# Gated linear attention: the state's products with the queries on four quarters of the array, a gate exponential put behind the next tile's decay logarithm, and the last output scaling on VectorE alone

## The chip, the cores and the metric

The kernel runs on one core of a Trainium2 chip. Its engines are TensorE (PE; PEld is its load of weights), VectorE (DVE), ScalarE (ACT), GpSimd (POOL) and SyncE (SP, which only issues DMAs here). The metric is the device time of one execution in microseconds: 2154.04 us before the change, the median of three runs (2153.7 to 2154.69).

## The reference

One layer of a decoder with two groups of heads side by side, for 2048 prompt tokens and 8 x 8 sample tokens: sliding-window attention (group A), gated linear attention (GLA, group B: 4 heads, key width 64, value width 128), an output projection, and a squared-ReLU MLP of width 4096, with RMSNorm before and after both halves. Cut to the part that the change touches:

```python
b = jnp.cumsum(log_a, axis=chunk)             # decays, within a chunk
k_rel = exp(where(causal, b_t - b_s, -inf)) * k_s
o_intra = einsum(einsum(q, k_rel), v)         # inside a chunk
q_dec, k_dec, a_blk = q * exp(b), k * exp(b_last - b), exp(b_last)
def step(S, xs):
    o = einsum('bthk,bhkv->bthv', q_dec, S)   # state times queries
    S = a_blk * S + einsum('bthk,bthv->bhkv', k_dec, v)
o = rms_norm(o_intra + o_inter, g_gla) * silu(gr)
...
x = x + rms_norm(f, g_ffn_post)               # the end of the layer
```

All inputs and outputs are float32.

## The kernel before

The work is cut into 16 tiles of 128 prompt tokens and one of 64 sample tokens, and goes in stages: the input projection of group A with its attention, GLA with its own input projection, the output projection, and two halves of the MLP, up and down, for 1024 tokens each. Large products are split into high and low parts that go through the array as fp32r, three products each; the small products of GLA are plain f32, and each of those leaves two matmul records in the trace.

**The GLA stage.** `gla(i, gp, og)` (from L1217) is a generator for tile i. Between its steps it yields a number of fill products; the loop at its caller then runs that many matmuls of the next tiles' projection (`gproj`), or of the output projection (`out`) at the end, from one list, so TensorE has work while the other engines prepare the tile. `G_FILL = (34, 14, 16, 8, 20)` gives these numbers. TensorE keeps the order in which the program issues its products.

For one tile, in the order of the program:

- `qk_T` (L1106) transposes queries and keys into PSUM bank "d". DVE copies the keys to `kt`; ACT copies the queries, scaled, into `qz`, which has two planes: plane r holds the queries of head r of a pair in 64 of 128 partitions, and zeros in the other 64.
- After 34 fills, seven `level_sums` (L1150) build decay sums on ACT (exponentials into `dec`) and DVE (sums in `before` and `after`), one for each of the block lengths 1 to 64; `weighted` (L1129) multiplies them into keys `XK` and queries `XQ`. The last level is issued behind the previous tile's masked copies (`put`). `dec[:, NL]` is the exponential of the whole tile's cumulated decay.
- `decayed(i + 1)` (L1210) starts the next tile: `log_decays` (L976) computes a small product z and on ACT its Abs, Exp and Ln.
- After 14 fills, `gate` (L1091) makes silu of the output gate: Abs, Exp and Ln on ACT, a DVE instruction, a last Exp on ACT (L1099), and two products on POOL.
- After 16 fills the decayed keys are transposed into bank "e" and copied by ACT to `kd`; then 8 fills.
- The scores of all levels (`gl`, `gh`), on two column halves of the array, then `ds`, the state's increment, also on two column halves, into bank "d". DVE computes `qd = qz * dec[:, NL]` (L1272), zeros included, copies the scores under masks into `AH`, and both engines copy them to `AT`. DVE updates the state S into its other buffer.
- After 20 fills, the output `o` in bank "e": for each head one product of `qd` (128 partitions, half of them zeros) and the state of its pair of heads, added to one product of `AT` and the values:

```python
o_ = bank([P, 4, P], "e", f"o_{i}")
for h in range(4):
    if i > 0:
        te.matmul(o_[:, h, :], qd[:, h % 2, h // 2], So[:, h // 2], start=True, stop=False)
    te.matmul(o_[:, h, :], AT[:, h, :], gv[:, h * P : (h + 1) * P], start=i == 0, stop=True)
```

- `finish_out` (L1178) squares, normalizes and gates `o` during the next tile, transposes it and stores it.

Most ACT and DVE instructions here are ordered by a scheduler when the program is built; `tc.issue_after(x)` puts those inside the block behind x on its engine.

**The end.** The last four token tiles leave their second halves ready (`prepare_last`). For each tile the last product is added to `f` (L2081); `square_last` (L2147) squares it on ACT and multiplies it by the gain; `finish_last` (L2155) makes the root on ACT (Ln, Exp), scales and adds the residual (L2165), and stores 512 columns at a time (L2166). The very last tile is handled in two pieces of 256 columns: the left piece is multiplied by the gain on POOL (L2151), scaled on ACT (L2162), added on POOL (L2163) and stored from ACT's queue (L2168); DVE and SP do the rest.

Of the kernel before, what the change touches and what calls it, by code (L numbers as in the profile page):

```python
# [15 lines left out]
AF = mybir.ActivationFunctionType  # L16
ALU = mybir.AluOpType
# [4 lines left out]
P = 128  # L22
# [3 lines left out]
NB = T // P  # L26
# [15 lines left out]
NL = len(LEVELS)  # L42
# [110 lines left out]
def hybrid_step_kernel(ctx: ExitStack, tc: tile.TileContext, I, O):  # L153
    nc = tc.nc
# [15 lines left out]
    def y_rows(i):  # L170
        return yp[i * P : (i + 1) * P, :] if i < NB else ys

    te, ac, dv = (InOrder(tc, engine) for engine in (nc.tensor, nc.scalar, nc.vector))
# [4 lines left out]
    def bank(shape, kind, name):  # L178

        return ps.tile(shape, F32, tag=kind, name=name, bufs=1 if kind in "de" else 2)  # L180
# [241 lines left out]
    half_of = slice(HD), slice(HD, P)  # L422
# [462 lines left out]
    for i in range(NB):  # L885
# [21 lines left out]
        if i >= NB - 2:  # L907
            t = i - NB + 2
# [60 lines left out]
    def ranks_T(pair, out):  # L969
        te.transpose(out, f32(glr[:, pair]).rearrange("p a r -> p (a r)"), ident)  # L970
        return out

    def first_ranks():
        ac.activation(glrT_first, ranks_T(0, bank([P, P], "b", "pg_0")), AF.Copy)

    def log_decays(i, z, t, gt, out):  # L976
        for g in range(2):
            te.matmul(z[:, g], wgk[:, i % 2, g * P : (g + 1) * P], gt[:, : z.shape[2]], start=True, stop=True)
        nc.scalar.activation(t, z, AF.Abs)
        nc.scalar.activation(t, t, AF.Exp, scale=-1.0)  # L980
        if out is not None:
            nc.scalar.activation(out, t, AF.Ln, bias=1.0)
        return z

    def first_decays():
# [44 lines left out]
    def places(name, shape, n=1, kind=F32):  # L1030
        return cycle([sp.tile(shape, kind, name=f"{name}{u}") for u in range(n)])
# [7 lines left out]
    XK = sp.tile([P, NL, 2, P], F32, name="XK")  # L1039
    XQ = sp.tile([P, NL, 2, 2, P // 2], F32, name="XQ")  # L1040
    sgs, prs = places("sg", [P, 512]), places("pr", [P, 256])
    qds = places("qd", [P, 2, 2, P])
    decs = places("dec", [P, NL + 1, 2, P])
    befores, afters = places("before", [P, 2, P]), places("after", [P, 2, P])
    kts = places("kt", [P, 2, P], 2)
# [45 lines left out]
    def gate(i, gp, n):  # L1091

        gr = gp[:n, 1024:1536]
        t = next(sgs) if n == P else s_sg
        nc.scalar.activation(t[:n], gr, AF.Abs)
        nc.scalar.activation(t[:n], t[:n], AF.Exp, scale=-1.0)
        nc.scalar.activation(t[:n], t[:n], AF.Ln, bias=1.0)
        nc.vector.scalar_tensor_tensor(t[:n], gr, 0.0, t[:n], op0=ALU.min, op1=ALU.subtract)
        nc.scalar.activation(t[:n], t[:n], AF.Exp)  # L1099
        engine = nc.vector if i in (0, NB) else nc.gpsimd  # L1100
        engine.tensor_tensor(t[:n], t[:n], gr, op=ALU.mult)
        t4 = t[:n].rearrange("p (h d) -> p h d", h=4)
        engine.tensor_tensor(t4, t4, ggla[:n].unsqueeze(1).to_broadcast([n, 4, P]), op=ALU.mult)
        return t
# [112 lines left out]
    def gla(i, gp, og=iter(())):  # L1217

        assert {(i, 0), (i, 1)} <= projected
        before, after = pre.pop(i)
        next(og, None)
        kt = qk_T(i, gp, P)
        dec = next(decs)
        following = decayed(i + 1) if i < NB - 1 else iter(())
        yield G_FILL[0] + 3 * (i == 1) if i else G_FIRST_FILL, True
        deque(og, 0)
        put_diagonal(i, AH, gp, P)
        for l, b in enumerate(LEVELS):  # L1230
            if l < (4 if i == 2 else NL - 1) or i == 0:
                level_sums(before, after, dec, l, b)
            else:
                with tc.issue_after(put[0].ins):
                    level_sums(before, after, dec, l, b)
            if l == NL - 1:
                kd = next(kds)
                pair = i // 2 + 1 if i % 2 == 0 and i < NB - 2 else 0
                turned = keys_decayed(after, kt, next(kdTs), P, "e", kd, pair)
                nc.scalar.activation(dec[:, NL], before, AF.Exp, scale=1.0 / 16)  # L1240
            weighted(XK, XQ, dec, kt, qz, l, b)
        next(turned)
        deque(following, 0)
        yield G_FILL[1] - 3 * (i == 1), True
        assert {(i, c) for c in range(4)} <= projected
        sg = gate(i, gp, P)
        yield G_FILL[2], True
        deque(turned, 0)
        yield G_FILL[3], True
        low = bank([P, 4, 4, P // 4], "c", f"gl_{i}")  # L1250
        high = bank([P, 512], "c", f"gh_{i}")
        mid = high[:, :256].rearrange("p (l h q) -> p l h q", l=2, h=4)
        far = high[:, 256:384].rearrange("p (r q) -> p r q", r=2)
        levels = [*(low[:, l] for l in range(4)), *(mid[:, l] for l in range(2))]
        for l, gm in enumerate(levels):
            for g in range(2):
                keys = XK[:, l, g] if l else kt[:, g]
                for u, uu in enumerate(half_of):
                    te.matmul(
                        gm[uu, 2 * g : 2 * g + 2], keys[:, uu], XQ[:, l, :, g, u * 32 : u * 32 + 32], start=True, stop=True  # L1260
                    )
        for g in range(2):
            te.matmul(far[half_of[g]], XK[:, NL - 1, g, :HD], XQ[:, NL - 1, :, g], start=True, stop=True)
        gv = gp[:, 512:1024]
        ds = bank([P, 2, P], "d", f"ds_{i}")
        for h in range(4):
            te.matmul(
                ds[half_of[h % 2], h // 2], kd[:, h * HD : (h + 1) * HD], gv[:, h * P : (h + 1) * P],
                start=True, stop=True,
            )  # L1270
        qd = next(qds)
        nc.vector.tensor_tensor(qd, qz, dec[:, NL].unsqueeze(1).to_broadcast([P, 2, 2, P]), op=ALU.mult)  # L1272
        for l, gm in enumerate(levels):
            put_level(AH, gm, msk[:, l], LEVELS[l])
        for g in range(2):
            nc.scalar.activation(AT[:HD, 2 * g : 2 * g + 2, HD:], far[half_of[g]], AF.Copy)
        put[:] = [nc.vector.tensor_copy(AT[half_of[1], :, half_of[1]], AH[half_of[1]])]
        done = nc.scalar.activation(AT[half_of[0], :, half_of[0]], AH[half_of[0]], AF.Copy)
        put.append(done)
        So, Sn = S[i % 2], S[(i + 1) % 2]  # L1280
        with tc.issue_after(put[0].ins):
            for g in range(2):
                nc.vector.scalar_tensor_tensor(
                    Sn[:, g], So[:, g], dec[:, NL, g, P - 1 : P], ds[:, g], op0=ALU.mult, op1=ALU.add
                )
        yield G_FILL[4], True
        o_ = bank([P, 4, P], "e", f"o_{i}")
        for h in range(4):
            if i > 0:
                te.matmul(o_[:, h, :], qd[:, h % 2, h // 2], So[:, h // 2], start=True, stop=False)  # L1290
            te.matmul(o_[:, h, :], AT[:, h, :], gv[:, h * P : (h + 1) * P], start=i == 0, stop=True)
        with tc.issue_after(done.ins):
            next(wo_parts, None)
        ogs_of[i] = og = finish_out(i, lambda h: o_[:, h, :], sg, P, "e")
        if i == NB - 1:
            yield from og
            for g in range(2):
                for r in range(2):
                    nc.sync.dma_start(O["gla_prompt"][0, 0, 2 * g + r], Sn[half_of[r], g])
# [847 lines left out]
    def square_last(i, fi, cc):  # L2147
        x1, fg, ssq = ending[i]
        left = cc.start == 0 and cc.stop < 512
        squares(i, fi[:, cc], cc, ssq[:, 1:2] if left else ssq[:, 0:1])  # L2150
        (nc.gpsimd if left else nc.vector).tensor_tensor(fg[:, cc], fi[:, cc], gpost[:, cc], op=ALU.mult)  # L2151
        if left:
            nc.vector.scalar_tensor_tensor(ssq[:, 2:3], ssq[:, 1:2], 1.0 / D, ssq[:, 2:3], op0=ALU.mult, op1=ALU.add)

    def finish_last(i):  # L2155
        x1, fg, ssq = ending[i]
        nc.scalar.activation(ssq[:, 3:4], ssq[:, 0:1], AF.Ln, scale=1.0 / D, bias=ssq[:, 2:3])
        nc.scalar.activation(ssq[:, 3:4], ssq[:, 3:4], AF.Exp, scale=-0.5)
        parts = [two, one]
        if i == NB - 1:  # L2160
            parts, left = [two, slice(256, 512)], slice(0, 256)
            nc.scalar.activation(fg[:, left], fg[:, left], AF.Copy, scale=ssq[:, 3:4])  # L2162
            nc.gpsimd.tensor_tensor(fg[:, left], fg[:, left], x1[:, left], op=ALU.add)  # L2163
        for dd in parts:
            nc.vector.scalar_tensor_tensor(fg[:, dd], fg[:, dd], ssq[:, 3:4], x1[:, dd], op0=ALU.mult, op1=ALU.add)  # L2165
            nc.sync.dma_start(y_rows(i)[:, dd], fg[:, dd])  # L2166
        if i == NB - 1:
            nc.scalar.dma_start(y_rows(i)[:, left], fg[:, left])  # L2168

    latest, newest = [], []  # L2170

# [277 lines left out]
```

## Time and profile before

| | |
|---|---|
| median of 3 runs | 2154.04 us |
| the profiled execution | 2154.72 us |
| its span | 2152.9 us |
| PE busy, matmul records | 2142.2 us, 11854 |
| PEld busy | 1860.6 us |
| DVE busy | 1528.0 us |
| ACT busy | 1220.5 us |
| POOL busy | 263.0 us |
| GLA stage, from the first tile's scores to the last tile's output | about 328 to 673 us |

The profile shows one execution. Busy time is the time in which an engine had at least one instruction at work; matmuls overlap, so a busy PE is not PE at its peak, and the distance from one start to the next says more than the length of one record. The chain of waits goes back from the last instruction to what released it, or to the instruction before it on its engine. In a row of a timeline stand the start, the length, the engine, the line, the operation, the tiles (out<-in), the shape and the count.

### The profile page before, as it was taken

The page shows a single profiled execution, that of the slowest core. Times are in us where ns is not written, and L with a number is a line of the kernel's source. Part 1 is how long each engine was busy: PE and PEld are TensorE (multiplying, and loading weights), DVE is VectorE, ACT ScalarE, POOL GpSimd, SP SyncE. Part 2 cuts the span into 40 slices and gives each one's busy share as a digit, 9 for nine tenths or more (in the row PEclk, how much of TensorE's full clock was granted, in tenths as well). Part 3 has the DMA queues.
Part 4 walks back from the last instruction along what each step waited for, and adds up shares of the span by engine and source line. Part 5 has one row for each costly group of instructions (what it writes and reads, how often), then busy time and mean ns, then how long its engine had stood idle before and what let it go on. Part 6 is the DMA issues. An engine that isn't in the chain of part 4 may idle for free.

```text
span 2152.9 us, 34347 instructions
## 1 busy us (share of the span) xinstructions
PE 2142.2 (100%) x11854; PEld 1860.6 (86%) x11854; DVE 1528.0 (71%) x3184; ACT 1220.5 (57%) x2628; POOL 263.0 (12%) x424
## 2 busy tenths in 40 slices
PE   9999999999999999999999999999999999999998
PEld 9999999999998888888888888888888888888887
DVE  7998878777775666988887555548766666555576
ACT  7998867566664444655555544345444445544454
POOL 4676511111111100000000000000000000000000
PEclk9999999999999999999999999999999999999999
DMA  7444341243427567777776877668544443766685
GB/s 243 157 145 145 103 118 46 86 138 114 157 100 272 189 207 240 247 258 274 260 274 218 263 246 224 209 199 275 176 170 162 152 158 125 260 204 192 193 273 177
DMA packets 241468, 411.55 MB, mean 191 GB/s; under 512 B 24893, under 2 KB 143405, under 8 KB 237181
## 3 DMA queue, kind: packets, MB, share of 16 engines
q1 hardware_dynamic: 240988, 408.95, 57.5%
q8 instruction: 94, 1.54, 0.3%
q14 instruction: 82, 0.66, 0.1%
q10 hardware_dynamic: 304, 0.40, 0.1%
HBM read 265.82 MB, written 143.99 MB: 190 GB/s over the span
## 4 chain that ended last, share of the span: by engine, by line
PE 96%; ACT 1%; DVE 1%; DMA 0%; issue 0%; POOL 0%; SPq 0%; DVEq 0%; POOLq 0%; ACTq 0%
PE dn L142 28%; PE gproj L142 13%; PE uc L142 8%; PE uX L142 8%; PE out L1423 7%; PE proj L142 6%; PE ud L142 4%; PE ue L142 4%; PE ub L142 4%; PE sam L142 2%; PE dsam L142 1%; PE o L142 1%; PE sc L142 1%; PE pT L142 1%; PE av L142 1%; PE gl L142 1%
## 5 line engine op out<-in xcount | busy, mean ns | idle before, releaser
L142 PE MATMUL dn<-o0t,o0s 128*128 128x512 f32 x888 | 345.4, 389 | 0.4 <-DVE f L2081 0.4
L142 PE MATMUL dn<-o0t,o1s 128*128 128x512 f32 x888 | 345.6, 389 | 0.0
L142 PE MATMUL dn<-o1t,o0s 128*128 128x512 f32 x888 | 345.5, 389 | 0.0
L2067 DVE TENSOR_TENSOR o1s<-rs,o0s 128x512 fp32r<-128x512 f32 x224 | 154.6, 691 | 222.4 <-ACT o0s L2066 219.4
L2066 ACT ACTIVATE o0s<-rs 128x512 fp32r<-128x512 f32 x224 | 141.2, 631 | 291.5 <-PE dn L142 255.8
L142 PE MATMUL gproj<-wg,gxh 128*128 128x384 f32 x1024 | 271.3, 341 | 0.2 <-ACT dec L1156 0.2
L142 ACT ACTIVATE st<-st 128x512 f32<-128x512 f32 x224 | 141.1, 630 | 101.7 <-DVE st L142 96.9
L142 PEld LDWEIGHTS dn<-o0t,o0s 128*128 128x128 f32 x888 | 166.8, 188 | 36.6 <-DVE f L2081 0.8
L142 PEld LDWEIGHTS dn<-o1t,o0s 128*128 128x128 f32 x888 | 166.7, 188 | 35.2
L142 PEld LDWEIGHTS dn<-o0t,o1s 128*128 128x128 f32 x888 | 166.7, 188 | 34.9
L142 PE MATMUL uc<-H,s 128*128 128x512 f32 x768 | 186.5, 391 | 0.0
L142 PEld LDWEIGHTS gproj<-wg,gxh 128*128 128x128 f32 x1024 | 183.8, 188 | 2.8 <-issue 1.9
L142 PE MATMUL gproj<-wg,gxl 128*128 128x384 f32 x576 | 185.9, 341 | 0.0
L142 PE MATMUL uX<-H,w 128*128 128x512 f32 x768 | 185.1, 390 | 0.0
L142 PEld LDWEIGHTS uX<-H,w 128*128 128x128 f32 x768 | 144.0, 188 | 30.3
L142 PEld LDWEIGHTS uc<-H,s 128*128 128x128 f32 x768 | 143.0, 188 | 30.6 <-ACT st L142 0.2
L1423 PE MATMUL out<-wo,mt 128*128 128x512 f32 x680 | 158.6, 392 | 0.0
L218 POOL TENSOR_TENSOR frs<-rs_v,half 128x1 f32<-128x1 f32 (+1 forms) x13 | 12.3, 952 | 1197.2 <-DVE rs_v L216 1197.2
L2067 DVE TENSOR_TENSOR o1t<-rt,o0t 128x512 fp32r<-128x512 f32 x222 | 152.1, 686 | 5.4 <-ACT o0t L2066 5.4
L1423 PEld LDWEIGHTS out<-wo,mt 128*128 128x128 f32 x680 | 126.5, 188 | 26.1
L2066 ACT ACTIVATE o0t<-rt 128x512 fp32r<-128x512 f32 x222 | 137.0, 619 | 10.9 <-DMA rt<-t_d 7.1
L142 DVE TENSOR_TENSOR st<-st 128x512 f32<-128x512 f32 x160 | 110.7, 692 | 30.1 <-ACT st L142 25.8
(440 smaller groups left out, 4314.3 us busy)
## 6 DMA issues: line engine op xcount, KB each, us to landing
s_d<-st SPq DMA_DIRECT2D x32, 1792.0 KB, 8.5
rs<-s_d SPq DMA_DIRECT2D x224, 256.0 KB, 3.4
raw<-in_w_up SPq DMA_DIRECT2D x64, 512.0 KB, 5.0
rt<-t_d SPq DMA_DIRECT2D x128, 256.0 KB, 3.8
rt<-in_w_down SPq DMA_DIRECT2D x96, 256.0 KB, 2.9
t<-in_w_down SPq DMA_DIRECT2D x64, 256.0 KB, 3.7
t_d<-t SPq DMA_DIRECT2D x32, 512.0 KB, 5.6
h_d<-ht SPq DMA_DIRECT2D x8, 1280.0 KB, 7.6
```

The source lines that it names most:

```text
L142: ins = call(*a, **k)
L218: return nc.gpsimd.tensor_tensor(out, v[:n], e, op=ALU.pow)
L1423: te.matmul(banks[c], x, w[:, c * 512 : (c + 1) * 512], start=k + u == 0, stop=k == KT - 1 and u == len(products) - 1,)
L2066: high = nc.scalar.activation(hi, raw, AF.Copy)
L2067: low = nc.vector.tensor_tensor(lo, raw, f32(hi), op=ALU.subtract)
```

## The change

Three things, all in the code printed above.

1. The products of state and queries. `qd` loses its zero half: DVE now makes it with two instructions, one for each 64 partitions, right behind `gate`. The products are eight of 64 x 64 (row half r is the head within a pair, column half u is half of the tokens, g the pair of heads), and stand behind `ds`, ahead of the 20 fills. Heads of row half 0 accumulate in bank "e", those of row half 1 in the second half of the bank "d" in which `ds` lies (`fourth`). The products of `AT` stay where they were and add to both. The transposes of `qk_T` move from bank "d" to "c".
2. Order on ACT and DVE. In tiles 1 to 14 the gate's last Exp is put behind the Ln of the latest `log_decays`. The last two levels, no longer only the last, are issued behind the previous tile's masked copies.
3. The end. The gain's product of the last tile is made once, 512 wide, on DVE, and the last scaling and store are as in the other tiles: two scalings and two stores of 512 columns, none on ACT or POOL.

```diff
@@ log_decays
-            nc.scalar.activation(out, t, AF.Ln, bias=1.0)
+            logged[:] = [nc.scalar.activation(out, t, AF.Ln, bias=1.0)]
@@ 
-    qds = places("qd", [P, 2, 2, P])
+    qds = places("qd", [P, 2, P])
@@ gate
-        nc.scalar.activation(t[:n], t[:n], AF.Exp)
+        with tc.issue_after(logged[0].ins) if 0 < i < NB - 1 else nullcontext():
+            nc.scalar.activation(t[:n], t[:n], AF.Exp)
@@ gla
-        kt = qk_T(i, gp, P)
+        kt = qk_T(i, gp, P, "c")
...
-            if l < (4 if i == 2 else NL - 1) or i == 0:
+            if l < (4 if i == 2 else NL - 2) or i == 0:
...
         sg = gate(i, gp, P)
+        qd = next(qds)
+        for r, rr in enumerate(half_of):
+            nc.vector.tensor_tensor(qd[rr], qz[rr, r], dec[rr, NL], op=ALU.mult)
...
-        ds = bank([P, 2, P], "d", f"ds_{i}")
+        fourth = bank([P, 4, P], "d", f"ds_{i}")
+        ds = fourth[:, :2]
...
-        qd = next(qds)
-        nc.vector.tensor_tensor(qd, qz, dec[:, NL].unsqueeze(1).to_broadcast([P, 2, 2, P]), op=ALU.mult)
+        So, Sn = S[i % 2], S[(i + 1) % 2]
+        o_ = bank([P, 2, P], "e", f"o_{i}"), fourth[:, 2:]
+        for g in range(2):
+            for u, uu in enumerate(half_of):
+                for r, rr in enumerate(half_of):
+                    if i > 0:
+                        te.matmul(
+                            o_[r][uu, g], qd[rr, g, uu], So[rr, g], start=g == 0, stop=False, skip_group_check=True
+                        )
...
         yield G_FILL[4], True
-        o_ = bank([P, 4, P], "e", f"o_{i}")
         for h in range(4):
-            if i > 0:
-                te.matmul(o_[:, h, :], qd[:, h % 2, h // 2], So[:, h // 2], start=True, stop=False)
-            te.matmul(o_[:, h, :], AT[:, h, :], gv[:, h * P : (h + 1) * P], start=i == 0, stop=True)
+            te.matmul(
+                o_[h % 2][:, h // 2], AT[:, h, :], gv[:, h * P : (h + 1) * P], start=i == 0, stop=True, skip_group_check=True
+            )
...
-        ogs_of[i] = og = finish_out(i, lambda h: o_[:, h, :], sg, P, "e")
+        ogs_of[i] = og = finish_out(i, lambda h: o_[h % 2][:, h // 2], sg, P, "e")
@@ square_last
-        (nc.gpsimd if left else nc.vector).tensor_tensor(fg[:, cc], fi[:, cc], gpost[:, cc], op=ALU.mult)
         if left:
             nc.vector.scalar_tensor_tensor(ssq[:, 2:3], ssq[:, 1:2], 1.0 / D, ssq[:, 2:3], op0=ALU.mult, op1=ALU.add)
+        else:
+            nc.vector.tensor_tensor(fg[:, one], fi[:, one], gpost[:, one], op=ALU.mult)
@@ finish_last
-        parts = [two, one]
-        if i == NB - 1:
-            parts, left = [two, slice(256, 512)], slice(0, 256)
-            nc.scalar.activation(fg[:, left], fg[:, left], AF.Copy, scale=ssq[:, 3:4])
-            nc.gpsimd.tensor_tensor(fg[:, left], fg[:, left], x1[:, left], op=ALU.add)
-        for dd in parts:
+        for dd in (two, one):
...
-        if i == NB - 1:
-            nc.scalar.dma_start(y_rows(i)[:, left], fg[:, left])
```

More of the change, by code (lines that the diff above doesn't have):

```diff
@@ L971, in ranks_T @@
         return out
+    logged = []
     def first_ranks():
@@ L1279, in gla @@
         put.append(done)
-        So, Sn = S[i % 2], S[(i + 1) % 2]
         with tc.issue_after(put[0].ins):
```

## The prediction

> **What bounds the kernel now.** I read the page first, then the busy time of the engines in the stretch that the change touches, then TensorE's own waits there, and last the chain of waits and the order of single matmuls in one tile.
>
> ```profile
> span 2152.9 us, 34347 instructions
> ...
> PE 2142.2 (100%) x11854; PEld 1860.6 (86%) x11854; DVE 1528.0 (71%) x3184; ACT 1220.5 (57%) x2628; POOL 263.0 (12%) x424
> ...
> PE 96%; ACT 1%; DVE 1%; DMA 0%; issue 0%; POOL 0%; SPq 0%; DVEq 0%; POOLq 0%; ACTq 0%
> ```
>
> TensorE (PE) is busy over the whole span and holds 96% of the chain that ended last. The profiled execution took 2154.72 us, 1.8 more than its span and 0.68 above the median of 2154.04; I make the sum as a difference and take it off the median. The stretch of gated linear attention, 328 to 673 us:
>
> ```profile
> 328.00:673.00 345.00, 344.96 (x2972) 331.50 (x2971) 264.39 (x787) 220.56 (x659) 60.58 (x60) 1.00 0.37 124
> ```
>
> ```profile
> PE gproj L142 <- ACT dec L1156: 0.2, 1, 0.2
> ```
>
> The first row gives the busy time of PE, PEld, DVE, ACT and POOL in these 345 us, then the granted clock of 1.00; the second is the only wait of PE from 320 to 680. PE is busy for 344.96 us, VectorE (DVE) for 264 and ScalarE (ACT) for 221. So an edit here is worth what it takes off PE's own stream, and edits on DVE and ACT are worth nothing unless they let PE wait.
>
> **What the state product costs now.** One tile in the chain of waits (start, length, matmul records; an f32 matmul leaves two):
>
> ```profile
> 509.89 0.70 PE gproj L142 x4
> 510.59 1.08 PE gl L142 x32
> ...
> 512.36 0.44 PE ds L142 x8
> 512.80 3.67 PE gproj L142 x20
> 516.47 1.78 PE o L142 x16
> ```
>
> A tile's o group is four products of state and queries and four of AT and values, 16 records in 1.78 us: 0.111 us a record. The eight of the state take 0.89 us. They run in 15 tiles (tile 0 has no state), which the count confirms:
>
> ```profile
> L142 PE MATMUL o<-S,qd 128*128 128x128 f32 x120 | 23.1, 274 | 0.0
> ```
>
> 120 records in 15 tiles are 15 x 0.89 = 13.4 us of PE. (The 23.1 us of this row counts overlapping records twice over with those of AT; the spacing is what counts.)
>
> **What it costs after.** Each tile gets eight products of 64 rows by 64 columns with 128 moving columns: two pair groups g, on four quarters of the array. That is 16 records, four for each quarter. What quarters do is read from neighbours that use halves:
>
> ```profile
> 510.08 0.51 PE L142 MATMUL gproj<-wg,gxh 128*128 128x384 f32 x2
> 510.52 0.45 PE L142 MATMUL gl<-XQ,kt 128*64 128x64 f32 x8
> 510.80 0.87 PE L142 MATMUL gl<-XQ,XK 128*64 128x64 f32 x24
> 511.50 0.86 PE L142 MATMUL gh<-XQ,XK 128*64 128x64 f32 x20
> 512.19 0.61 PE L142 MATMUL ds<-gp,kd 128*64 128x128 f32 x8
> 512.73 0.45 PE L142 MATMUL gproj<-wg,gxl 128*128 128x384 f32 x1
> 513.01 0.51 PE L142 MATMUL gproj<-wg,gxh 128*128 128x384 f32 x2
> ```
>
> ds is eight records of 128 columns on two column halves, and the chain above gives them 0.44 us: 0.109 us for a round of two, as long as a full-array record takes alone. So column halves run side by side. Four side by side are seen in the sample's scores, which lie on four column strips of 32:
>
> ```profile
> 283.00 0.44 PE L142 MATMUL ssc<-kc,qs 64*32 64x128 f32 x8
> 283.24 0.31 PE L142 MATMUL ssc<-kns,qs 64*32 64x64 f32 x8
> 283.48 0.45 PE L142 MATMUL gproj<-wg,gxl 128*128 128x384 f32 x1
> ```
>
> From 283.00 to 283.48 there are eight records of 128 columns and eight of 64. One after another they would need 8 x 0.109 plus 8 x 0.058 (the 24 gl records take 0.70 from 510.80 to 511.50, 0.058 a round) = 1.34 us; in rounds of four 2 x 0.109 + 2 x 0.058 = 0.33, and the 0.48 that passed hold a change of mode too. So strips work as four independent streams. If quarters do the same, the 16 records are four rounds: 4 x 0.109 = 0.44 us. What the trace doesn't show is two row halves at once; that is the main uncertainty.
>
> A change of array shape costs something as well. In the group above gproj follows gproj by 0.175 us (four in 0.70 in the chain), so after the pair that starts at 510.08 gl would follow at 510.43; it starts at 510.52, 0.09 later. Its first eight records take 0.28 us where the later ones take 0.233, another 0.05. Out of it, ds should end at 512.19 + 0.44 = 512.63; gproj starts at 512.73, and its next one 0.28 later where 0.175 is usual, 0.10 twice. Now ds (128 x 64) would be followed by quarters (64 x 64), a switch more in each tile; the way back to gproj is paid already. The same two shapes follow each other once, in the other direction:
>
> ```profile
> 372.23 0.68 PE L142 MATMUL s_oi<-s_at,gp_s 64*64 64x64 f32 x16
> 372.84 0.29 PE L142 MATMUL s_oe<-s_qz,s 128*64 128x16 f32 x4
> ```
>
> s_oi is 16 records of 64 columns, eight rounds of 0.058 and 0.05 for the first: its end is at 372.23 + 0.52 = 372.75, and s_oe starts at 372.84, 0.09 later. So I price the switch at 0.09 plus 0.05 for the first round, 0.14 us; bounds 0.09 (no slow first round) and 0.20 (as the way back to gproj).
>
> The Trainium skill, page "TensorEngine Tiling (Array Packing)", section "Tiling Modes", says that changing the tiling mode, not just the tile, drains TensorE; this speaks against the change. The trace agrees, with the 0.09 us at each of these places, and its drain is in the sum.
>
> Per tile: 0.89 off, 0.44 + 0.14 on, 0.31 us gained; over 15 tiles 4.7 us. With the bounds of the switch 3.8 to 5.4 us. Another bound: a round of gl takes 0.058 us, loads of 64 weight columns included; if the loads of the two row halves queue in one column half, a round of quarters takes 2 x 0.058 = 0.117 instead of 0.109, 0.5 us over all tiles.
>
> **Does PE wait anywhere new?** The quarters stand right behind ds, ahead of the 20 fill products (3.67 us) that stood before them. They need qd, the state, and the banks. The state was written in the tile before. qd is on DVE:
>
> ```profile
> L1272 DVE TENSOR_TENSOR qd<-qz,dec x16: 678/689/693, 326.1 to 655.1; 128x512 f32<-128x512 f32 x16
> ```
>
> ```profile
> L1135 DVE TENSOR_TENSOR XQ<-dec,qz x73: 415/422/445, 436.6 to 654.8; 128x256 f32<-128x256 f32 x73
> ```
>
> One instruction of 0.69 us becomes two of half the size, 0.69 to 0.84 together by these rows, and stands behind the gate in the tile, 24 fill products ahead of its use; DVE idles 80 us in the stretch. Cost nothing; if it came late, PE would wait for its length at most. The bank of o's first half held the transposed decayed keys, which ACT copies out to kd before ds anyway:
>
> ```profile
> 533.05 0.36 ACT L1146 ACTIVATE kd<-kdT 128x256 f32<-128x256 f32 x1
> ```
>
> ```profile
> 533.67 0.61 PE L142 MATMUL ds<-gp,kd 128*64 128x128 f32 x8
> ```
>
> In this tile the copy ends at 533.41 and ds starts at 533.67: 0.26 us of room, the tightest place that I found. The change reorders two things ahead of that copy on ACT. The gate's last exponential goes behind the next tile's decay logarithm:
>
> ```profile
> 526.22 0.63 ACT L1099 ACTIVATE sg<-sg 128x512 f32<-128x512 f32 x1 [0.28 <-DVE sg L1098]
> ```
>
> Here ACT idled 0.28 us for DVE's part of the gate while that logarithm stood behind it. After the change the logarithm runs first, so the level sums start earlier by up to the 0.63 us of that exponential, and the copy with them; queued behind the exponential on ACT are the level exponentials, and POOL waits for it with the gate's two products, which the next tile's output scaling needs. Also one level more of the sums is put behind the masked copies. Both give room, so I take nothing. AT is safe too:
>
> ```profile
> 515.57 0.40 ACT L1278 ACTIVATE AT<-AH 64x256 f32<-64x256 f32 x1
> ```
>
> ```profile
> 516.52 0.39 PE L142 MATMUL o<-gp,AT 128*128 128x128 f32 x2
> ```
>
> AT is ready at 515.97 and first used at 516.52. With the quarters ahead (0.58 us) and the first two state records gone (0.22 us), it is used 0.36 us later after ds than now. The transposes of queries and keys go from bank d to c, whose last readers are done before AT. Bank d, which now keeps o's second half, is next taken by the following decay product, and that stands on PE behind the transposes of the scaled output, so behind o's last reader. None of this adds a wait to PE.
>
> **The tail.** It is a chain without PE. For the third last tile and the last two:
>
> ```profile
> 2141.34 1.42 DVE L2165 SCALAR_TENSOR_TENSOR lfg<-lfg,lssq,lx 128x512 f32<-128x512 f32 x2 [0.63 <-ACT lssq L2158]
> ```
>
> ```profile
> 2144.83 1.89 DVE L2165 SCALAR_TENSOR_TENSOR lfg<-lfg,lssq,lx 128x512 f32<-128x512 f32 x2
> ...
> 2146.71 0.41 DVE L2081 TENSOR_TENSOR f<-f,dn 128x256 f32<-128x256 f32 x1
> ...
> 2148.32 1.65 DVE L2165 SCALAR_TENSOR_TENSOR lfg<-lfg,lssq,lx 128x512 f32<-128x512 f32 x2 [0.74 <-ACT lssq L2158]
> ```
>
> ```profile
> 2144.99 1.18 POOL L2151 TENSOR_TENSOR lfg<-f,gfpost 128x256 f32<-128x256 f32 x1 [72.97 <-DVE f L2081]
> ```
>
> ```profile
> 2145.97 0.28 PE L142 MATMUL dn<-o0t,o1s 128*128 128x256 f32 x1
> ```
>
> The pair of scalings takes 1.42 us when alone and 1.89 beside POOL's product, so the last addition starts at 2146.71 although PE ended at 2146.25. Without POOL the pair ends at 2146.25 and the addition can start at about 2146.32, 0.39 earlier. The gain's product becomes 512 wide, 0.69 instead of 0.42, but the square, its sum and two small activations lie beside it (2146.71 + 0.41 to 2148.32, 1.20 us). Then the last pair takes 1.42 for both halves instead of 1.65 for one half and a quarter beside POOL: ready 0.62 earlier. Against that the last store doubles:
>
> ```profile
> DMA to landing us min/median/max: 2.1/2.1/2.1
> ```
>
> ```profile
> 2149.99 0.33 SPq L2166 DMA_DIRECT2D out_y_prompt<-lfg  x1
> ```
>
> ```profile
> SPq L2445 <- DMA out_y_prompt<-lfg: 1.5, 1, 1.5
> ```
>
> 256 KB land in 2.1 us; the last 128 KB took 0.33 us to issue at 2149.99, and the queue then waited 1.5 us for them at the end, 1.8 at least. So 0.1 to 0.3 us more for 256 KB. I take 0.4 us gained (bounds 0.2 and 0.6).
>
> **Sum.** 4.7 + 0.4 = 5.1 us: 2154.04 - 5.1 = 2148.9 us. By the bounds 3.5 to 6.0: 2148.0 to 2150.5 is this case's own range. A change of this kernel under about 0.2%, 4.3 us, can hardly be told from none.
>
> **Rivals.** (1) The row halves take turns, column halves run together as in ds: eight rounds, 0.87 + 0.14 = 1.01 against 0.89, 0.12 us worse per tile, 1.8 us, less the tail: 2155.4, slower than before. It decides from 6.8 rounds on (0.89 - 0.14 over 0.109). For it: no row shows two row halves at work together. Against it: the four strips of the scores behave as independent streams, and the two halves write to different banks. Chance 0.10. The Trainium skill, page "TensorE: Matmul & The Clock Gate", section "Part 3: Packing small matmuls", has row and column groups run together with about 4 ns between starts, which is the forecast's case; no run here shows it for rows.
> (2) Quarters run singly: 16 x 0.109 + 0.14 = 1.88, 0.99 worse per tile, 2168.5. Against it stand ds and the scores. Chance 0.02.
> (3) A wait takes the place: the reordered ACT puts the gate's 0.63 us ahead of the kd copy in most tiles; less the 0.26 of room 0.37 us in some 14 tiles, 5.2 us, the gain gone: 2154.1. Slower from 0.6 us a tile on. The rows on the gate speak against it. Chance 0.05.
> (4) Quarters overlap, but the mode changes or the weight loads cost more than their bounds, 0.10 to 0.20 us a tile: 2150.5 to 2151.9. Chance 0.08.
>
> **How the numbers follow.** The forecast has 0.75. Faster by over 0.2% means under 2149.7: most of the forecast's case, 0.62. Within 0.2%: the rest of it, rivals 1 and 4, half of 3: 0.34. Slower: rival 2 and a part of 3, 0.04. The range goes from 2147.9 to 2151.7, from the forecast's case through most of rival 4; outside are rivals 1 to 3 and the edges.
>
> **What would show it.** Right: the o group after a tile falls to 0.89 us with eight records; behind ds stand 16 records of 64 x 64 by 128 columns with a first start 0.09 late and starts in fours, ending within 0.6 us; PE's waits from 320 to 680 stay under 1 us; the tile period shrinks by 0.31 us; the last pair of scalings takes 1.42 us. Wrong: quarter records in pairs 0.109 apart with eight rounds; a PE wait on kd, qd or AT; gproj's restart later than the 0.10 and 0.28 of now.

## The result and the profile after

The change makes the kernel slower: 2160.68 us (median of 9 runs, 2158.48 to 2164.53) against 2154.47 for the kernel before (9 runs, 2153.70 to 2156.27). The ratio is 1.0027, 95% interval 1.0018 to 1.0036. The forecast was 2148.9, with a range from 2147.9 to 2151.7. The profiled execution took 2159.29 us.

The page of the kernel after, its span, busy times and chain by engine:

```profile
span 2157.5 us, 34608 instructions
...
PE 2140.3 (99%) x11974; PEld 1853.2 (86%) x11974; DVE 1546.5 (72%) x3200; ACT 1223.8 (57%) x2627; POOL 259.5 (12%) x422
...
PE 86%; DVE 6%; ACT 4%; issue 2%; POOL 1%; DMA 1%; DVEq 0%; ACTq 0%; POOLq 0%
```

PE's share of the chain that ended last has fallen from 96% to 86%: DVE and ACT now stand in it. The busy times of 328 to 673 us, for PE, PEld, DVE, ACT and POOL:

```profile
328.00:673.00 345.00, 337.08 (x3062) 318.94 (x3061) 282.06 (x799) 221.69 (x653) 59.83 (x60) 1.00 0.37 121
```

In the same 345 us PE was idle for 0.04 us before and is idle for 7.92 now, at the same clock, while DVE is busy for 17.7 us more. PE's waits from 320 to 680 us in the kernel after say for what:

```profile
PE ds L142 <- ACT kd L1149: 6.5, 9, 1.5
PE s_oi L142 <- DVE s_at L1169: 1.0, 1, 1.0
PE o L142 <- ACT AT L1292: 0.3, 1, 0.3
PE gproj L142 <- ACT dec L1159: 0.2, 1, 0.2
```

In nine tiles the list has a wait of the state's increment `ds` for ACT's copy of the decayed keys, `kd`: the place that the prediction called the tightest. (The list counts only time in which no matmul record is at work. By the starts of the records, `ds` comes later than its 1.67 us after the tile's first score in twelve of the tiles 1 to 14.) The quarters themselves do what was forecast. PE's timeline in tile 2, where `ds` doesn't wait:

```profile
377.65 0.61 PE L142 MATMUL ds<-gp,kd 128*64 128x128 f32 x8
378.18 0.32 PE L142 MATMUL o<-S,qd 64*64 64x128 f32 x1
378.19 0.32 PE L142 MATMUL ds<-S,qd 64*64 64x128 f32 x1
378.20 0.32 PE L142 MATMUL o<-S,qd 64*64 64x128 f32 x1
378.20 0.32 PE L142 MATMUL ds<-S,qd 64*64 64x128 f32 x1
378.34 0.27 PE L142 MATMUL o<-S,qd 64*64 64x128 f32 x1
...
378.45 0.27 PE L142 MATMUL o<-S,qd 64*64 64x128 f32 x1
...
378.56 0.27 PE L142 MATMUL o<-S,qd 64*64 64x128 f32 x1
...
378.78 0.45 PE L142 MATMUL gproj<-wg,gxl 128*128 128x384 f32 x1
```

`ds` ends at 377.65 + 0.44 = 378.09, and the first quarter starts 0.09 us later. Four quarters start within 0.02 us, and the rounds follow at 378.34, 378.45 and 378.56: 0.16, then 0.11 twice. With 0.11 for the last, the quarters take 0.58 us from 378.09. That is the forecast's 0.44 + 0.14.

**Where the time came from.** The next timelines show DVE, POOL and ACT around the scores of tile 8, which start at 511.98 in the kernel after and at 510.52 before. The gate and the key copy `kd` are tile 8's there; the decay logarithm and the level sums are already tile 9's, because all levels but the last ones are worked on while the tile before is still at its scores. First DVE in the kernel after, from the decay logarithm's last step (`before<-z,zt`) to the first level sums:

```profile
507.39 0.43 DVE L1091 SCALAR_TENSOR_TENSOR before<-z,zt 128x256 f32<-128x256 f32 x1
507.85 1.36 DVE L1162 TENSOR_TENSOR after<-after,before 128x128 f32<-128x128 f32 x1
509.31 1.28 DVE L1163 TENSOR_TENSOR before<-before 128x128 f32<-128x128 f32 x1
510.69 0.29 DVE L1162 TENSOR_TENSOR after<-after,before 128x128 f32<-128x128 f32 x1
```

POOL of the kernel after in the same time, the gate's two products:

```profile
507.77 1.30 POOL L1104 TENSOR_TENSOR sg<-sg,gp 128x512 f32<-128x512 f32 x1 [6.02 <-ACT sg L1102]
509.14 1.30 POOL L1106 TENSOR_TENSOR sg<-sg,ggla 128x512 f32<-128x512 f32 x1
```

A level sum takes 0.29 us. The one that starts 0.08 us behind POOL's first product takes 1.36 and ends at 509.21, 0.14 after that product; the next takes 1.28 and ends 0.15 after the second product. The third, with POOL idle, takes 0.29 again. So two sums cost 2.06 us more than they should. The same stretch before, DVE first, then POOL:

```profile
506.43 0.42 DVE L1089 SCALAR_TENSOR_TENSOR before<-z,zt 128x256 f32<-128x256 f32 x1 [1.76 <-ACT zt L982]
506.88 0.82 DVE L1159 TENSOR_TENSOR after<-after,before 128x128 f32<-128x128 f32 x1
507.62 0.41 DVE L1172 SCALAR_TENSOR_TENSOR pr<-gp 128x256 f32<-128x256 f32 x1
507.96 0.28 DVE L1160 TENSOR_TENSOR before<-before 128x128 f32<-128x128 f32 x1
```

```profile
504.88 1.30 POOL L1101 TENSOR_TENSOR sg<-sg,gp 128x512 f32<-128x512 f32 x1 [5.21 <-ACT sg L1099]
506.26 1.29 POOL L1103 TENSOR_TENSOR sg<-sg,ggla 128x512 f32<-128x512 f32 x1
```

Before, the first product ran while DVE sat idle for 1.76 us, and only the end of the second met a sum: 0.82 instead of 0.29, ending 0.15 after the product. Note the row at 506.43: it runs beside POOL for its whole length and takes its usual 0.42. One of its inputs, z, is in PSUM, while both inputs of the sums are in SBUF. The Trainium skill, page "SBUF — State Buffer", section "Who interferes with whom", has DVE and GpSimd share one pair of SBUF ports under an exclusive lock: a DVE instruction with two SBUF inputs contends with a GpSimd instruction that reads SBUF, and one with at most one SBUF input, outside DVE's two-port modes, doesn't. The trace agrees, with 0.82, 1.36 and 1.28 us for the sums against 0.42 for the row at 506.43.

The change moves the gate's last exponential from ahead of the logarithm to just behind it, so POOL gets its work when DVE starts on the sums. ACT in the kernel after, and PE's transposes of the decayed keys (`kdT`), show how that comes to the key copy:

```profile
507.00 0.62 ACT L1102 ACTIVATE sg<-sg 128x512 f32<-128x512 f32 x1
...
509.30 0.32 ACT L1161 ACTIVATE dec<-after 128x128 f32<-128x128 f32 x1 [1.13 <-DVE after L1162]
...
510.62 0.32 ACT L1159 ACTIVATE dec<-before 128x128 f32<-128x128 f32 x1 [0.53 <-DVE before L1163]
...
514.63 0.37 ACT L1149 ACTIVATE kd<-kdT 128x256 f32<-128x256 f32 x1
```

```profile
510.17 0.38 PE L142 MATMUL kdT<-ident,kdT 128*128 128x128 f32 x2
```

The level exponentials wait for the blocked sums, `kd` stands behind them in ACT's queue, and `ds` waits for `kd`. The copy needs none of these exponentials, which belong to tile 9: its own input, the transposed keys, was complete at 510.55, 4.1 us before the copy starts. Only its place in ACT's queue ties it to the sums. Level sums over 0.6 us between 320 and 680 us number 11 before and 24 after, counted in the two traces.

### The profile page after: what moved, and what is told of

Its sections match the earlier page's. It is cut to its first block, busy times and chain, and to the rows that moved or that the text cites. A ratio compares the mean times of both kernels' runs of the same rounds, so it can differ in the third digit from the quotient of the medians.

```text
span 2157.5 us, 34608 instructions
## 1 busy us (share of the span) xinstructions
PE 2140.3 (99%) x11974; PEld 1853.2 (86%) x11974; DVE 1546.5 (72%) x3200; ACT 1223.8 (57%) x2627; POOL 259.5 (12%) x422
## 4 chain that ended last, share of the span: by engine, by line
PE 86%; DVE 6%; ACT 4%; issue 2%; POOL 1%; DMA 1%; DVEq 0%; ACTq 0%; POOLq 0%
PE dn L142 28%; PE uc L142 8%; PE uX L142 8%; PE out L1435 7%; PE gproj L142 6%; PE proj L142 6%; PE ud L142 4%; PE ue L142 4%; PE ub L142 4%; PE sam L142 1%; PE dsam L142 1%; PE sc L142 1%; DVE after L1162 1%; PE pT L142 1%; PE av L142 1%
```

## The experiments

The kernels ran in three groups of four, in the order of the table, each group on one chip together with the kernel before, whose medians there were 2154.11, 2153.81 and 2153.52 us. Ratios are to these.

| kernel | median us | ratio to before (95%) |
|---|---|---|
| exponential free | 2155.33 | 1.0008 (0.9999 to 1.0016) |
| levels back | 2158.53 | 1.0018 (1.0009 to 1.0027) |
| no gate products | 2148.10 | 0.9973 (0.9962 to 0.9983) |
| before, exponential moved | 2160.57 | 1.0030 (1.0019 to 1.0041) |
| both orders back | 2152.25 | 0.9993 (0.9984 to 1.0002) |
| before, level moved | 2154.71 | 1.0005 (0.9996 to 1.0013) |
| gate products on DVE | 2147.72 | 0.9971 (0.9959 to 0.9982) |
| gain moved | 2149.45 | 0.9979 (0.9970 to 0.9988) |
| row halves, products on DVE | 2153.53 | 0.9998 (0.9989 to 1.0008) |
| quarters, products on DVE, orders back | 2148.02 | 0.9971 (0.9960 to 0.9982) |
| POOL products cut in two | 2152.19 | 0.9994 (0.9985 to 1.0003) |
| before, tail alone | 2152.68 | 0.9996 (0.9987 to 1.0005) |

**The first four: which part of the change costs.** T1 is the theory above, T2 blames the second level behind the masked copies, T3 the exponential's own time on ACT.

*Exponential free.* After with

```diff
-        with tc.issue_after(logged[0].ins) if 0 < i < NB - 1 else nullcontext():
-            nc.scalar.activation(t[:n], t[:n], AF.Exp)
+        nc.scalar.activation(t[:n], t[:n], AF.Exp)
```

> The changed kernel with one part undone: the gate's last exponential is again free to run ahead of the next tile's decay logarithm. Theory 1 (the exponential's new place lets POOL's two gate products fall on the level sums, which then take 1.3 us instead of 0.3 on DVE; the kd copy stands behind the level exponentials on ACT, and ds waits for it): the ds waits of 6.5 us go, two long level sums a tile become one or none, and the time is about 2149.5 us (2148.5 to 2151). Theory 2 (the second level put behind the masked copies makes the wait): no difference, about 2160 us. Theory 3 (it is the exponential's own 0.62 us on ACT ahead of the level exponentials, POOL has no part in it): as theory 1.

2155.33 us: about 5 of the 11 us that the kernel after lies above T1's 2149.5 are back, not all, so T1 was incomplete. Long sums are down to 10, yet PE's waits still hold

```profile
PE ds L142 <- ACT kd L1148: 4.9, 6, 1.5
```

*Levels back.* After with `NL - 1` in place of `NL - 2`.

> The changed kernel with only the last level behind the masked copies, as before; the gate's exponential stays behind the decay logarithm. Theories 1 and 3: the ds waits stay, 2159 to 2164 us. Theory 2: they go, about 2149.5 us.

2158.53 us, 25 long sums, and nine waits for `kd` are left (4.8 us): the level's place isn't the main cause.

*No gate products.* After with POOL's two products left out in tiles 1 to 14, so the gate lacks its input and its gain there:

```diff
+        if i in (0, NB - 1, NB):
             engine.tensor_tensor(t[:n], t[:n], gr, op=ALU.mult)
             ...
```

> The changed kernel without POOL's two gate products in tiles 1 to 14 (the product with the gate's input and with the gain are left out, nothing is put in their place). The exponential stays behind the logarithm. Theory 1: the level sums take 0.3 us each again, ds waits at most 1 us in all, 2149 to 2150 us. Theory 3: the waits stay nearly whole, 2157 us or more. Theory 2: the waits stay, about 2160 us.

2148.10 us, no sum over 0.6 us. The waits on `kd`, `s_at` and AT are gone, and of PE's waits from 320 to 680 us there is left

```profile
PE gproj L142 <- ACT dec L1160: 0.2, 1, 0.2
```

Both order changes are still in this kernel. So neither the exponential's 0.62 us on ACT (T3) nor the level (T2) costs anything once POOL's products are away.

*Before, exponential moved.* Before with the exponential behind the logarithm, nothing else.

> The kernel before with one part of the change alone: the gate's last exponential behind the next tile's decay logarithm. Theories 1 and 3: ds waits for kd appear, and the kernel gets slower by 6 to 11 us, 2160 to 2165. Theory 2: no difference, 2154 us.

2160.57 us: this one move alone gives the slowdown, with 24 long sums and seven waits of `ds` for `kd`. Levels back, 2158.53 in the same group, is the same order with the quarters and the new tail. It is only 2.0 us faster, where these were forecast at 5.1: as far as the chain to `kd` sets the pace, PE's shorter tile is worth nothing.

**The next four: what is left without the move.** Theory A: each order change lengthens the chain to `kd`. Theory B: that chain is longer than PE's shortened tile anyway.

*Both orders back.* The two edits above together: quarters and tail alone.

> After with both order changes undone: the gate's last exponential free again, and six of the seven levels ahead of the masked copies again. The quarters and the last scaling on VectorE stay. Theory A (the exponential's place, which puts GpSimd's gate products on the level sums, and the second level behind the masked copies each lengthen the chain of VectorE and ScalarE to the key copy): 2148.5 to 2150.5, no tensor matmul waiting for the key copy. Theory B (that chain is longer than TensorE's shortened tile of 21.18 us by itself, whatever the order): 2152 to 2155, with the state's update waiting for the key copy from tile 7 on as in the kernel with the exponential free.

2152.25 us, nearer to B. The sums are as in before (10 long ones), PE's tile is shorter, and so `ds` waits where it had room:

```profile
PE ds L142 <- ACT kd L1148: 1.5, 3, 0.8
```

*Before, level moved.* Before with `NL - 2` in place of `NL - 1`.

> Before with the second level put behind the masked copies, and nothing else of the change. Theory A: the second level costs by itself, since its exponentials stand on ScalarE behind the projection copy (0.58 us) and the weight copy (1.05 us) and the last level's sums wait for them; before had 0.06 to 0.85 us of room a tile, so 2155 to 2159 with TensorE waiting for the key copy. Theory B: the level's place costs nothing, 2154 within 1 us, no wait.

2154.71 us, not distinguishable from before by the median. In the trace `ds` comes 0.39 and 0.28 us late in tiles 13 and 14; with PE's longer tile the level's place costs little more than that.

*Gate products on DVE.* After with one line changed:

```diff
-        engine = nc.vector if i in (0, NB) else nc.gpsimd
+        engine = nc.vector
```

> After with the gate's two products on VectorE in place of GpSimd, the exponential still behind the logarithm and the second level still behind the masked copies. If the loss is VectorE's blocked sums (1.3 in place of 0.29 us, twice a tile, some 2.0 us): VectorE pays two products of about 0.68 us, 1.36 us a tile, in their place, so about a third less of a delay and 2154 to 2159. If the exponential's own 0.62 us on ScalarE were the loss: no better than after, 2160 to 2163. If the products on VectorE stand in front of the sums in its queue and wait there for the exponential: 2161 to 2166.

2147.72 us, better than any of the three expectations and faster than both kernels. DVE in its tile 8:

```profile
502.66 0.29 DVE L1162 TENSOR_TENSOR after<-after,before 128x128 f32<-128x128 f32 x1
502.87 0.69 DVE L1104 TENSOR_TENSOR sg<-sg,gp 128x512 f32<-128x512 f32 x1
503.48 0.28 DVE L1163 TENSOR_TENSOR before<-before 128x128 f32<-128x128 f32 x1
503.68 0.68 DVE L1106 TENSOR_TENSOR sg<-sg,ggla 128x512 f32<-128x512 f32 x1
504.28 0.42 DVE L1175 SCALAR_TENSOR_TENSOR pr<-gp 128x256 f32<-128x256 f32 x1
```

The products take 0.69 and 0.68 us on DVE instead of 1.30 each on POOL, and they lie between sums, where DVE partly waits for ACT's exponentials in any case. I had counted their 1.36 us as delay against the blocked sums' 2.06; the room of the key copy, 1.0 to 2.6 us in tiles 1 to 14, shows that most of it was none.

*Gain moved.* Both orders back, and the gain taken off POOL: it becomes the scale of ACT's copy of the turned output in tiles 1 to 14.

```diff
-        engine.tensor_tensor(t4, t4, ggla[:n].unsqueeze(1).to_broadcast([n, 4, P]), op=ALU.mult)
+        if not 0 < i < NB - 1:
+            engine.tensor_tensor(t4, t4, ggla[:n].unsqueeze(1).to_broadcast([n, 4, P]), op=ALU.mult)
...
-            nc.scalar.activation(mo[:, :, :n], pt[:, :, :n], AF.Copy)
+            nc.scalar.activation(mo[:, :, :n], pt[:, :, :n], AF.Copy, scale=glacol if 0 < i < NB else 1.0)
```

> Both order changes undone, quarters and last scaling kept, and in tiles 1 to 14 the product with the gain is taken off GpSimd: the gain becomes the scale of ScalarE's copy of the turned output, in which it is one number a partition, so one GpSimd product of 1.29 us is left and it ends ahead of the level sums. Theory A: 2147.5 to 2149.5, TensorE's own floor (2148.1 with both products left out). Theory B: 0.5 us of blocked sums less a tile than with both order changes undone alone, 2148 to 2151, and 1 to 4 us below that kernel.

2149.45 us: one product ends ahead of the sums, no long sum, no wait for `kd`. Theory A's upper end, though both theories allow it.

**The last four: what blocks, and what each part is worth.**

*Row halves, products on DVE.* Before with the two order changes and the products on DVE.

> Before, with the two order changes and the gate's products on VectorE, but the state product still as row halves beside the score product and the last scaling as before. It differs from the kernel with all of the change and the products on VectorE (2147.72) by the quarters and the last scaling alone. If those are worth the 4.7 and 0.4 us of the prediction: 2152.3 to 2153.7, TensorE's own tile of 21.49 to 21.59 us, no wait for the key copy. If the quarters save less than that and the products on VectorE gave the rest: 2149 to 2151.

*Quarters, products on DVE, orders back.* After with the products on DVE, the exponential free and `NL - 1`.

> Quarters and last scaling kept, the gate's products on VectorE, both order changes undone. Theory C (GpSimd's products are the whole loss: a VectorE sum that meets one waits until it ends, and without that the chain to the key copy is shorter than TensorE's 21.18 us in either order): 2147.2 to 2148.6, no wait for the key copy. If the orders are needed to stay under 21.18 us: 2149 to 2152, with such waits. The key copy's room was 1.0 to 2.2 us with the orders of the change; without the logarithm ahead of the exponential I expect 0.3 to 1.6.

2153.53 and 2148.02 us in the same group. The first shows that products on DVE, even with the change's orders, are worth nothing without the quarters: PE's own stream binds there, and 1.4 us or more of room at `kd` is unused. The second has the orders of before and is as fast as the kernel with the orders of the change (2147.72). So the difference of the two, 5.5 us, is put down to quarters and tail, forecast at 5.1, although the orders differ as well. The room in the second is 0.2 to 1.3 us in tiles 5 to 13 and gone in tile 14 (0.1 us of delay): the orders give room, as the prediction said, but no time. It also corrects theory B: the chain to `kd` is too long for PE's shortened tile only with POOL's products in it.

*POOL products cut in two.* After with each product in two instructions of 256 columns.

```diff
-        engine.tensor_tensor(t[:n], t[:n], gr, op=ALU.mult)
...
+        cuts = (slice(0, 2), slice(2, 4)) if 0 < i < NB else (slice(0, 4),)
+        for hh in cuts:
+            cc = slice(hh.start * P, hh.stop * P)
+            engine.tensor_tensor(t[:n, cc], t[:n, cc], gr[:, cc], op=ALU.mult)
...
```

> After, with each of the gate's two products on GpSimd cut into two of 256 columns, nothing else. If a VectorE sum waits for the end of the one GpSimd instruction that it meets: no sum over 0.9 us (0.65 and the 0.15 that a sum ends behind the product), more of them, and 2155 to 2160. If the two engines share a rate while GpSimd has anything to do: sums of 1.2 us and over as in after, and 2160 to 2163.

2152.19 us, lower than I expected. Its DVE in tile 8, then its POOL (two instructions to a row):

```profile
504.00 0.79 DVE L1167 TENSOR_TENSOR after<-after,before 128x128 f32<-128x128 f32 x1
504.89 0.65 DVE L1168 TENSOR_TENSOR before<-before 128x128 f32<-128x128 f32 x1
505.64 0.65 DVE L1167 TENSOR_TENSOR after<-after,before 128x128 f32<-128x128 f32 x1
506.21 0.95 DVE L1180 SCALAR_TENSOR_TENSOR pr<-gp 128x256 f32<-128x256 f32 x1
```

```profile
503.90 1.49 POOL L1108 TENSOR_TENSOR sg<-sg,gp 128x256 f32<-128x256 f32 x2 [6.00 <-ACT sg L1102]
505.35 1.53 POOL L1111 TENSOR_TENSOR sg<-sg,ggla 128x256 f32<-128x256 f32 x2
```

Four POOL instructions of about 0.75 us block four DVE instructions, three sums (0.65 to 0.79) and `pr`, each for one of them. The longest of all sums is 0.83 us where it was 1.40: a DVE instruction waits for the end of the one that it meets, and the engines don't share a rate. The blocked DVE time in this tile is (0.79 + 0.65 + 0.65 - 3 x 0.29) + (0.95 - 0.42) = 1.75 us, not much below 2.06. Over all tiles the difference is larger: what the sums take above 0.29 us each from 320 to 680 us adds up to 22.4 us in the kernel after and to 16.5 here, 5.9 less, and the stretch from tile 0's first score to tile 15's is 6.3 us shorter. That the two figures are close fits a kernel paced by this chain; it wasn't followed tile by tile.

*Before, tail alone.* Before with the change's last scaling.

> Before with the last scaling of the change alone. 2153.4 by the prediction's 0.4 us (0.2 to 0.6), which the median can't tell from before; the trace can: from the last matmul's end to the end of the span 0.2 to 0.6 us less than in before, and the last scaling on VectorE near 1.4 in place of 1.9 us a pair.

2152.68 us, not distinguishable from before by the median. From the end of the last matmul to the end of the span it takes 6.12 us where before takes 6.69.

## Why the prediction was wrong

**What was right.** The state product: 0.89 us off and 0.58 on, as measured above; rivals 1, 2 and 4 are out. The Trainium skill, page "TensorE: Matmul & The Clock Gate", section "Part 3: Packing small matmuls", has about 4 ns between the starts of groups, which no row showed for row halves then; the trace agrees, with four starts from 378.18 to 378.20. From tile 0's first score to tile 15's, PE needs 335.27 us before and 330.67 with the products on DVE, worked out from the starts of the records: 4.60 for 14 tiles, 0.33 a tile against 0.31. (That kernel gains 6.1 us on before in its group. The 4.6 and the tail's 0.56 make 5.2. Most of the rest lies outside the stretch: in the profiled execution the first score starts at 327.02 us instead of 328.53. That start lies between 327.0 and 328.5 us in all the kernels here, changed or not, so the rest isn't put down to the change.) The tail, with DVE of the kernel after, PE's last record there and SyncE's wait at the end:

```profile
2149.96 1.41 DVE L2173 SCALAR_TENSOR_TENSOR lfg<-lfg,lssq,lx 128x512 f32<-128x512 f32 x2
...
2151.41 0.42 DVE L2093 TENSOR_TENSOR f<-f,dn 128x256 f32<-128x256 f32 x1
...
2153.04 1.41 DVE L2173 SCALAR_TENSOR_TENSOR lfg<-lfg,lssq,lx 128x512 f32<-128x512 f32 x2 [0.47 <-ACT lssq L2171]
```

```profile
2151.10 0.28 PE L142 MATMUL dn<-o0t,o1s 128*128 128x256 f32 x1
```

```profile
SPq L2451 <- DMA out_y_prompt<-lfg: 1.6, 1, 1.6
```

The pairs take 1.41 us and the last addition starts at 2151.41, 0.03 us after PE's end at 2151.38 (before: 0.46 us after it). From there to the end of the span it is 6.1 us against 6.7: 0.56 gained, forecast 0.4 (0.2 to 0.6). The last store is waited for 1.6 us instead of 1.5, at the low end of what was set against the gain.

**What failed** is the step "Does PE wait anywhere new?", at its end: the level sums "start earlier by up to the 0.63 us of that exponential, and the copy with them", "Both give room, so I take nothing". The sums do start earlier: tile 9's first one starts 4.13 us ahead of tile 8's scores (507.85 against 511.98), where it was 3.64 before (506.88 against 510.52). But the copy doesn't come earlier with them. Three things were wrong in the step.

The first and largest: the step saw that POOL waits for the exponential with the gate's two products, but asked only who needs their result, not what they run beside. They run beside the level sums, which have to wait for them. This is the effect that the same prediction priced in the tail, where a scaling pair took 1.89 us beside POOL and 1.42 alone; the step didn't carry it over to a place where POOL's work was being moved. From tile 0's first score to tile 15's the kernel after takes 341.55 us, 10.9 more than the same kernel with the products on DVE. 8.6 of these lie between the scores and `ds` (33.64 against 25.04 us in tiles 0 to 14; the list of waits has 6.5 for them, as it counts only time without any record at work), 1.1 between `ds` and AT's products, 1.1 in the one place where the sample's products wait for DVE, and 0.1 within AT's products. The gain of 4.6 and this loss of 10.9 make the 6.3 us by which the stretch grew.

The second: the room of 0.26 us at `kd` was read at PE's old pace and then taken as if it stayed, although the change itself takes 0.31 us from each of PE's tiles. Nor was it the tightest place: in the same trace the copy of tile 7 ends 0.23 us ahead of `ds`, and that of tile 3 0.06 (399.97 against 400.03). With both orders undone the kernel gains 1.6 us on before; in the same group the one with the products on DVE, in which the waits for `kd` are gone, gains 6.1. So even the forecast's own gain needed that chain shortened first.

The third: the level behind the masked copies was to give room too. With POOL's products in place it takes room. By the stretch from tile 0's first score to tile 15's, one execution each, it costs 0.8 us alone on before (336.03 against 335.27), 1.7 beside the moved exponential (341.55 against 339.81) and 3.4 with the exponential free (337.72 against 334.34).

Rival 3 had the right place, and its threshold holds: it was to turn slower from 0.6 us a tile on, and 10.9 us are 0.78 for each of 14 tiles. Its cause was wrong: it charged ACT with the exponential's 0.63 us, and without POOL's products that exponential is still there while PE doesn't wait for `kd` at all. The sign was named beforehand: a PE wait on `kd` was listed under "wrong".

**What stays open.** The medians alone can't confirm what the second level behind the masked copies costs: alone on before they show no difference, and between the kernel with the exponential free (1.0008) and that with both orders back (0.9993) the intervals just overlap, though the waits on `kd` grow from 1.5 to 4.9 us. With the products on DVE it costs nothing. A more direct cure wasn't tried: `kd` ahead of the next tile's level exponentials in ACT's queue, since its input is complete 2.1 to 4.6 us before it starts in tiles 1 to 14 of the kernel after.

## What to carry to other kernels

When an instruction moves, follow everything that it releases, on every engine, and ask what those run beside, not only who needs their result. A room read in a trace belongs to that trace's pace: take from it what the change itself saves on the engine that binds. The cure that worked here was found by asking which engine the released work should be on: two products of 1.3 us on POOL were 0.7 each on DVE, and in gaps there.

## What the runs showed of the hardware

- An f32 sum of two SBUF tiles on DVE, 0.29 us alone, takes 1.26 to 1.40 us when it starts up to 0.18 us behind the start of a POOL product of 1.30 us: it ends about 0.15 us after the product, whatever is left of that. The product itself keeps its 1.30 us in most tiles.
- Four 64 x 64 products of 128 moving columns in f32 run side by side in 0.11 us, with starts within 0.02 us, as long as one record on the whole array; the change from 128 x 64 costs 0.09 us and the first round 0.05 more.
